# Seven half-size products for both feed-forward outputs, over neighbouring block pairs, three of them inside the input stage

## The chip, the core and the metric

The kernel runs on one core of a Trainium2 chip. The metric is the device time of one execution in microseconds. Engines are TensorE (PE, matmuls and weight loads), VectorE (DVE), ScalarE (ACT), GpSimd (POOL) and SyncE (SP, which issues most DMAs). Each engine takes its instructions in the order in which the program lists them and waits on semaphores for others. POOL and ACT can issue DMAs too.

## The reference

One layer over 512 tokens of width 1024 (D), with a feed-forward width FF of 2816 = 22 blocks of 128, all in fp32:

```python
mod = silu(c) @ w_ada + b_ada
sh1, sc1, g1, sh2, sc2, g2, sh3, sc3, g3 = split(mod, 9)
swiglu = lambda u, w_in, w_out: (silu(a) * b) @ w_out      # a, b = split(u @ w_in, 2)

u = rms_norm(x, ffn1_norm_g) * (1 + sc1) + sh1
x = x + 0.5 * g1 * swiglu(u, ffn1_w_in, ffn1_w_out)
u = rms_norm(x, mix_norm_g) * (1 + sc2) + sh2
merged = mix(u)               # mLSTM branch and forgetting attention, gated
x = x + g2 * (merged @ w_out)
u = rms_norm(x, ffn2_norm_g) * (1 + sc3) + sh3
x = x + 0.5 * g3 * swiglu(u, ffn2_w_in, ffn2_w_out)
```

## The kernel before

Every fp32 operand of a matmul is split into a high part (made by ACT, a copy to the matmul's type) and a low part (made by DVE, the difference). Each product is then three matmuls: high x high, low x high, high x low (`mm3`, L112 to L114; L93 and L95 split weights). Tiles ending in h and l, as wh and wl, are these parts. A weight tile is loaded by SP into raw, split, and used once. A matmul of 128x512 is the usual piece.

The stages, one after another: start (modulation rows 0 and 1, first norm, and blocks 0 to 2 of FFN1's input product), FFN1's input product for blocks 3 to 21, FFN1's output product, the mix, the branches, w_out, FFN2.

**FFN1.** `ffn_in` makes for each block j the two halves a and b (48 matmuls), then `ffn_h` makes silu(a) * b and stores its high and low part (hh, hl) in memory for all 22 blocks. `token_gemm` then computes the output in two halves of 512 columns: for each, 22 blocks x 4 token blocks x 3 matmuls. While this runs, x stays in its eight tiles, and `residual` adds to it. `ada_row` computes a row of the modulation on DVE (8 products of a 128x1024 weight, then a small matmul); rows 2 to 6 run as `extra` beside FFN1's input product, rows 7 and 8 beside its output product. The second norm's first half (`norm_half(0)`) runs in the last part of `token_gemm`, its second half behind it.

**FFN2** already uses seven half-size products (the Strassen-Winograd form of a 2x2 by 2x2 block product). The token rows are cut in two halves, the hidden blocks in pairs (j, j + 11), the output columns in two halves. With A the hidden values (A12: first token half, second block) and B the weights (B12: first block, second column half), sums are formed:

```
S1 = A21 + A22   S2 = S1 - A11   S3 = A21 - A11   S4 = A12 - S2
T1 = B12 - B11   T2 = B22 - T1   T3 = B12 - B22   T4 = B21 - T2
```

and the products are A11 B11, A12 B21, S1 T1, S2 T2, S4 B22, S3 T3, A22 T4. `pair_sums` forms the S on DVE, `weight_sums` the T: it loads the pair's two weight rows (tile rw, two buffers each 512 KB), splits B11 and B21, forms T1 and T2 with their parts and T3 and T4, and stores them to DRAM (T_d). A11 B11 and A12 B21 run inside the pairs (`first_products`, 12 matmuls a pair). The five others run behind the last pair in `ffn_out`, each 66 matmuls x 2 half-size outputs (`product`), with the T read back, T1 and T2 already split (`w_ready`). x stays in its tiles throughout.

The order on each engine follows the program's order as a scheduler laid it out; the names in the tables below are the program's, with a running number.

Of the kernel before, what the change touches and what calls it, by code (L numbers as in the profile page):

```python
# [20 lines left out]
P = 128  # L21
# [27 lines left out]
class Layer:  # L49
# [168 lines left out]

    def xn_start(self, pool):
        return [pool.tile([P, 512], F32, name=self.nm("xn"), tag="xs", bufs=8) for h in range(2)]  # L220
# [36 lines left out]
    def norm_half(self, hf, pool, G, sh):  # L257

        nc = self.nc
        if hf == 0:  # L260
            self.u_tiles()
        xn = self.xnorm(hf, pool)

        b = [self.tbank() for _ in range(4)]
        for k in range(NK):
            for i in range(2):
                nc.tensor.transpose(b[k % 4][:, k // 4 * 256 + i * P:k // 4 * 256 + (i + 1) * P],
                                    xn[i][k // 4][:, k % 4 * P:(k % 4 + 1) * P], self.ident)
        for k in range(NK):
            self.u_from(b[k % 4][:, k // 4 * 256:(k // 4 + 1) * 256], k, hf * 256, 256, G[:, k:k + 1], sh[:, k:k + 1], pool)  # L270
# [8 lines left out]
    def ada_row(self, v, pool, bank):  # L279

        nc, A = self.nc, self.A
        acc = pool.tile([P, D], F32, name=self.nm("acc"), tag="xn", bufs=2)
        br = pool.tile([1, D], F32, name=self.nm("br"), tag="xn", bufs=2)
        for k in range(NK):
            r = self.raw([P, D], [(lambda t: t, A["w_ada"][0, k * P:(k + 1) * P, v * D:(v + 1) * D])])
            if k == 0:
                nc.sync.dma_start(br, A["b_ada"][:, v * D:(v + 1) * D])
                with self.tc.issue_after(self.last_ul.ins):
                    nc.vector.tensor_scalar(acc, r, self.ccol[:, 0:1], None, op0=MUL)
            else:  # L290
                nc.vector.scalar_tensor_tensor(acc, r, self.ccol[:, k:k + 1], acc, op0=MUL, op1=ADD)  # L291
            if k == NK - 1:

                t = self.wp.tile([P, D], F32, name=self.nm("fo"), tag="wh", bufs=4)
                hl = self.wp.tile([P, D], F32R, name=self.nm("hl"), tag="wl", bufs=4)
                nc.scalar.activation(t[0:64, :], acc[64:P, :], AF.Copy)
                nc.vector.tensor_tensor(acc[0:64, :], acc[0:64, :], t[0:64, :], op=ADD)
                nc.scalar.activation(hl[0:64, :], acc[0:64, :], AF.Copy)
                nc.vector.tensor_tensor(hl[64:P, :], acc[0:64, :], hl[0:64, :], op=SUB)
                for h in range(2):  # L300
                    b = bank()
                    s = slice(h * 512, (h + 1) * 512)
                    nc.tensor.matmul(b[0:1, :], self.oneR, hl[:, s], start=True, stop=True)
                    nc.vector.tensor_tensor(br[:, s], b[0:1, :], br[:, s], op=ADD)
                nc.sync.dma_start(self.mod_d[v:v + 1, :], br)
            yield
# [20 lines left out]
    def ffn_h(self, ps_a, ps_b, j, c0, c1, hp, tp):  # L327
        nc = self.nc
        w = c1 - c0
        s = self.tmp(tp, "sl")  # L330
        nc.scalar.activation(s[:, :w], ps_a[:, c0:c1], AF.Silu)
        nc.vector.tensor_tensor(s[:, :w], ps_b[:, c0:c1], s[:, :w], op=MUL)
        nc.scalar.activation(self.hh[j][:, c0:c1], s[:, :w], AF.Copy)
        nc.vector.tensor_tensor(self.hl[j][:, c0:c1], s[:, :w], self.hh[j][:, c0:c1], op=SUB)

    def h_tiles(self, hp):
        self.hh = [hp.tile([P, T], F32R, name=self.nm("hh"), tag=f"hh{j}", bufs=1) for j in range(NJ)]
        self.hl = [hp.tile([P, T], F32R, name=self.nm("hl"), tag=f"hl{j}", bufs=1) for j in range(NJ)]

    def ffn_in(self, w_in, j0, hp, tp, extra=None):  # L340
        for j in range(j0, NJ):
            pa, pb = self.gbank(), self.gbank()
            self.gemm_stat(pa, self.w_stat(w_in, j * P), 0, T)
            self.gemm_stat(pb, self.w_stat(w_in, FF + j * P), 0, T)
            self.ffn_h(pa, pb, j, 0, T, hp, tp)
            self.lo_after = None
            if extra:
                extra(j)

    def ffn_in_halves(self, w_in, nj, hp, tp):  # L350

        wa = [self.w_stat(w_in, j * P) for j in range(nj)]
        wb = [self.w_stat(w_in, FF + j * P) for j in range(nj)]
        pp = [(self.gbank(), self.gbank()) for _ in range(nj)]
        for h in range(2):
            for j in range(nj):
                c0, c1 = h * 256, (h + 1) * 256
                self.gemm_stat(pp[j][0], wa[j], c0, c1)
                self.gemm_stat(pp[j][1], wb[j], c0, c1)
                self.ffn_h(pp[j][0], pp[j][1], j, c0, c1, hp, tp)  # L360

    def sum_tiles(self, hp):

        self.hc = {n: hp.tile([P, NP, 256], F32, name=self.nm(n), tag="hc", bufs=4) for n in ("S1", "S2", "S3", "A22")}
        self.s4 = [hp.tile([P, NP, 256], F32R, name=self.nm("s4"), tag=f"s4{i}") for i in range(2)]
        self.T_d = [self.dp.tile([NP * P, 1024], F32, name=self.nm("T_d")) for _ in range(3)]
        self.pair = {}

    def hidden(self, ps_a, ps_b, j, c0, c1, hp, tp):

        nc = self.nc
        jj, o = j % NP, 2 * (1 - j // NP)
        if jj not in self.pair:
            self.pair[jj] = hp.tile([P, 4, 256], F32, name=self.nm("hp"), tag="hp", bufs=2)
        h = self.pair[jj].rearrange("p c t -> p (c t)")[:, o * 256 + c0:o * 256 + c1]
        s = self.tmp(tp, "sl")
# [3 lines left out]
    def pair_sums(self, jj, hp):  # L380

        nc, V, h = self.nc, self.nc.vector, self.pair[jj]
        A12, A22, A11, A21 = (h[:, c, :] for c in range(4))
        c = {n: t[:, jj, :] for n, t in self.hc.items()}
        V.tensor_tensor(c["S1"], A21, A22, op=ADD)
        V.tensor_tensor(c["S2"], c["S1"], A11, op=SUB)
        V.tensor_tensor(c["S3"], A21, A11, op=SUB)
        nc.scalar.activation(c["A22"], A22, AF.Copy)
        hi = hp.tile([P, 2, 256], F32R, name=self.nm("ha"), tag="ha", bufs=2)
        lo = hp.tile([P, 2, 256], F32R, name=self.nm("la"), tag="la", bufs=2)  # L390
        nc.scalar.activation(hi, h[:, 0::2, :], AF.Copy)
        V.tensor_tensor(lo, h[:, 0::2, :], hi, op=SUB)
        V.tensor_tensor(A12, A12, c["S2"], op=SUB)
        nc.scalar.activation(self.s4[0][:, jj, :], A12, AF.Copy)
        V.tensor_tensor(self.s4[1][:, jj, :], A12, self.s4[0][:, jj, :], op=SUB)
        self.pair[jj] = (hi, lo)

    def weight_sums(self, w, jj, hp):

        nc, V = self.nc, self.nc.vector  # L400
        sh = [P, 1024]
        r1, r2 = (hp.tile(sh, F32, name=self.nm("rw"), tag="rw", bufs=2) for _ in range(2))
        nc.sync.dma_start(r1, w[jj * P:(jj + 1) * P, :])
        nc.sync.dma_start(r2, w[(jj + NP) * P:(jj + NP + 1) * P, :])
        B11, B12, B21, B22 = r1[:, 0:512], r1[:, 512:], r2[:, 0:512], r2[:, 512:]
        tiles = lambda: (self.wp.tile([P, 2, 512], F32R, name=self.nm("wh"), tag="wh", bufs=4),
                         self.wp.tile([P, 2, 512], F32R, name=self.nm("wl"), tag="wl", bufs=4))
        wh, wl = tiles()
        for i, B in enumerate((B11, B21)):
            nc.scalar.activation(wh[:, i, :], B, AF.Copy)  # L410
            V.tensor_tensor(wl[:, i, :], B, wh[:, i, :], op=SUB)
        self.pair[jj] += (wh, wl)
        V.tensor_tensor(B11, B12, B11, op=SUB)
        V.tensor_tensor(B12, B12, B22, op=SUB)
        V.tensor_tensor(B22, B22, B11, op=SUB)
        V.tensor_tensor(B21, B21, B22, op=SUB)
        th, tl = tiles()
        for i, B in enumerate((B11, B22)):
            nc.scalar.activation(th[:, i, :], B, AF.Copy)
            V.tensor_tensor(tl[:, i, :], B, th[:, i, :], op=SUB)  # L420
        rows = slice(jj * P, (jj + 1) * P)
        for d, t in zip(self.T_d, (th, tl)):
            nc.sync.dma_start(d[rows, :], t.rearrange("p i n -> p (i n)").bitcast(F32))
        nc.sync.dma_start(self.T_d[2][rows, 0:512], B12)
        nc.sync.dma_start(self.T_d[2][rows, 512:], B21)
# [18 lines left out]
    def product(self, ps, A, W, first, tail=0):  # L444
# [14 lines left out]
        for part in body:  # L459
            ops = (*A(*part), *W(*part))  # L460
            for t in range(2):
                run(t, part, ops)
# [840 lines left out]
```

## Time and profile before

| what | us |
|---|---|
| median of 3 runs (1366.8 to 1372.09) | 1367.05 |
| the profiled execution | 1370.4 |
| its span | 1368.6 |
| PE busy in the span | 1337.8 |
| start stage ends, FFN1's block 3 begins | 72.9 |
| FFN1's output product | 283.6 to 410.0 |
| branch stage | 876.0 to 964.5 |
| FFN2's pairs and closing products | 1011 to 1368.6 |

The span is the time from the first to the last instruction of the profiled execution; the 1.8 us beside it lie around it. PE is busy in all but 30.8 us of it, nearly half of which (14.6) lie in the first 76 us.

### The profile page before, as it was taken

How to read it: one execution, taken by the hardware profiler on the slowest of the kernel's cores; microseconds unless marked ns; L12 is line 12 of the kernel's file. 1: busy time of each engine (PE TensorE's matmuls, PEld its weight loads, DVE VectorE, ACT ScalarE, POOL GpSimd, SP SyncE). 2: the span in 40 equal slices, each digit the busy share in tenths (PEclk: the TensorE clock that was granted, in tenths of full speed). 3: DMA queues.
4: the chain of work that ended last, by engine and by line, in shares of the span. 5: the costliest groups of instructions: out<-in, count | busy, mean ns of one | idle time of the engine just before them, and what ended most of it. 6: DMA issues, size and time to landing. Idle time of an engine off the chain costs nothing.

```text
span 1368.6 us, 17759 instructions
## 1 busy us (share of the span) xinstructions
PE 1337.8 (98%) x6504; PEld 1118.9 (82%) x6504; DVE 874.2 (64%) x1567; ACT 596.8 (44%) x1034; POOL 115.4 (8%) x143
## 2 busy tenths in 40 slices
PE   6899999999999999999999999899999999999998
PEld 5788887888779888888888878788888888888787
DVE  6666666655548767867595876446566555565646
ACT  4433333322235755456465675332353333333343
POOL 2000000000002010313130411002010000000000
PEclk9899999999999999999999999999999999999999
DMA  9466666655634334343333253355326656556774
GB/s 315 134 200 191 184 198 206 217 188 179 223 85 104 117 101 131 112 131 120 108 101 112 81 154 94 92 166 174 126 74 218 213 162 223 185 188 212 245 274 150
DMA packets 226763, 221.92 MB, mean 162 GB/s; under 512 B 12082, under 2 KB 179666, under 8 KB 226676
## 3 DMA queue, kind: packets, MB, share of 16 engines
q1 hardware_dynamic: 226196, 220.71, 51.9%
q8 instruction: 51, 0.84, 0.2%
q14 instruction: 36, 0.29, 0.1%
q0 software_dynamic: 416, 0.06, 0.0%
q10 hardware_dynamic: 64, 0.02, 0.0%
HBM read 192.89 MB, written 27.86 MB: 161 GB/s over the span
## 4 chain that ended last, share of the span: by engine, by line
PE 85%; DVE 8%; ACT 3%; DMA 3%; issue 1%; SPq 0%; POOL 0%; POOLq 0%; DVEq 0%; ACTq 0%
PE g L114 21%; PE g L112 21%; PE g L113 21%; PE t L112 2%; PE t L113 2%; PE t L114 2%; PE g L709 2%; PE t L1051 2%; DVE wl L95 1%; PE t L456 1%; PE t L457 1%; PE t L455 1%; PE t L1021 1%; DMA wl<-T_d 1%; PE t L992 1%
## 5 line engine op out<-in xcount | busy, mean ns | idle before, releaser
L95 DVE TENSOR_TENSOR wl<-raw,wh 128x1024 fp32r<-128x1024 f32 (+2 forms) x217 | 275.7, 1271 | 185.6 <-ACT wh L93 164.5
L93 ACT ACTIVATE wh<-raw 128x1024 fp32r<-128x1024 f32 (+2 forms) x217 | 226.1, 1046 | 336.4 <-PE g L113 140.6
L114 PE MATMUL g<-uh,wl 128*128 128x512 f32 (+2 forms) x984 | 369.7, 376 | 2.1 <-DVE wl L95 2.1
L112 PE MATMUL g<-uh,wh 128*128 128x512 f32 (+2 forms) x984 | 370.8, 377 | 0.1
L113 PE MATMUL g<-ul,wh 128*128 128x512 f32 (+2 forms) x984 | 369.7, 376 | 0.0
L114 PEld LDWEIGHTS g<-uh,wl 128*128 128x128 f32 (+1 forms) x984 | 184.6, 188 | 37.3 <-DVE wl L95 3.3
L112 PEld LDWEIGHTS g<-uh,wh 128*128 128x128 f32 (+1 forms) x984 | 184.7, 188 | 34.1 <-ACT wh L93 1.1
L113 PEld LDWEIGHTS g<-ul,wh 128*128 128x128 f32 (+1 forms) x984 | 184.8, 188 | 33.6
L112 PE MATMUL g<-wh,uh 128*128 128x512 f32 (+1 forms) x320 | 111.8, 349 | 0.0
L114 PE MATMUL g<-wh,ul 128*128 128x512 f32 (+1 forms) x320 | 111.1, 347 | 0.0
L113 PE MATMUL g<-wl,uh 128*128 128x512 f32 (+1 forms) x320 | 111.0, 347 | 0.0
L291 DVE SCALAR_TENSOR_TENSOR acc<-raw,ccol,acc 128x1024 f32<-128x1024 f32 x49 | 62.8, 1282 | 13.0 <-DMA raw<-in_w_ada_dram 12.3
L112 PEld LDWEIGHTS g<-wh,uh 128*128 128x128 f32 x320 | 60.5, 189 | 7.8 <-DVE tk L905 0.5
L114 PEld LDWEIGHTS g<-wh,ul 128*128 128x128 f32 x320 | 60.5, 189 | 7.8
L113 PEld LDWEIGHTS g<-wl,uh 128*128 128x128 f32 x320 | 60.5, 189 | 7.4
L112 PE MATMUL g<-yh,wh 128*128 128x512 f32 x128 | 50.1, 395 | 3.7 <-ACT yh L1110 3.7
L254 POOL TENSOR_TENSOR ul<-uf,uh 128x256 fp32r<-128x256 f32 x16 | 13.5, 846 | 456.0 <-DVE uf L253 456.0
L114 PE MATMUL g<-yh,wl 128*128 128x512 f32 x128 | 50.5, 395 | 0.0
L113 PE MATMUL g<-yl,wh 128*128 128x512 f32 x128 | 50.3, 393 | 0.0
L378 DVE TENSOR_TENSOR hp<-g,sl 128x512 f32<-128x512 f32 (+1 forms) x24 | 15.4, 646 | 51.5 <-PE g L114 50.9
L1003 ACT ACTIVATE S<-S,mn 128x128 f32<-128x128 f32 (+1 forms) x64 | 35.6, 557 | 22.5 <-DVE mn L995 14.8
L984 POOL TENSOR_TENSOR Am<-A,maskF 128x512 f32<-128x512 f32 x16 | 24.0, 1500 | 136.4 <-DMA A<-A_d 133.6
(316 smaller groups left out, 2215.1 us busy)
## 6 DMA issues: line engine op xcount, KB each, us to landing
raw<-in_ffn_w_in_dram SPq DMA_DIRECT2D x82, 512.0 KB
raw<-in_w_ada_dram SPq DMA_DIRECT2D x56, 512.0 KB
raw<-in_w_mix_dram SPq DMA_DIRECT2D x48, 512.0 KB
raw<-in_ffn_w_out_dram SPq DMA_DIRECT2D x27, 512.0 KB
rw<-in_ffn_w_out_dram SPq DMA_DIRECT2D x22, 512.0 KB
raw<-in_w_mix_dram SPq DMA_DIRECT2D x32, 256.0 KB
ar<-in_w_ada_dram SPq DMA_DIRECT2D x14, 512.0 KB
T_d<-rw SPq DMA_DIRECT2D x22, 256.0 KB
```

The lines of the kernel that those rows point to most:

```text
L93: nc.scalar.activation(hi, src, AF.Copy)
L95: self.last_lo = (eng or nc.vector).tensor_tensor(lo, src, hi, op=SUB)
L112: mm(ps, lh, rh, start=start, stop=False)
L113: mm(ps, lh, rl, start=False, stop=False)
L114: self.last_mm = mm(ps, ll, rh, start=False, stop=stop)
L291: nc.vector.scalar_tensor_tensor(acc, r, self.ccol[:, k:k + 1], acc, op0=MUL, op1=ADD)
L378: nc.vector.tensor_tensor(h, ps_b[:, c0:c1], s[:, :c1 - c0], op=MUL)
L455: mm(ps[t], a[0], wh[:, k, :], start=first and c + k == 0, stop=False, skip_group_check=True)
L709: mm = nc.tensor.matmul(acc_ps[b], (wl if p == 1 else wh)[:, b % 2, s], ul if p == 2 else uh, start=k == 0 and p == 0, stop=k == NK - 1 an ...
L984: nc.gpsimd.tensor_tensor(b4(Am), b4(A0), self.maskF[:, None, :].to_broadcast([P, NT, P]), op=ADD)
L1003: nc.scalar.activation(S[:, ws], S[:, ws], AF.Exp, scale=-1.0, bias=m, accum_out=sm[:, qb:qb + 1])
L1051: nc.tensor.matmul(po[:, q0:], vt[pr][:, kb, i % 2, :], Px[:, o:o + T - q0], start=n == 1, stop=n == 8)
```

## The change

Both FFNs now go through one path. FFN1's output becomes seven half products (462 matmuls for 528), and in both the pair is (2jj, 2jj + 1), so that a pair is complete one block after the other.

- `first_products` runs three products per pair inside the input stage (18 matmuls): S1 T1 is added to the two. Its operands ah, al, s1, th, tl take the eight tiles of x. FFN1 therefore fetches x again from the input, FFN2 stores x to x_d before its pairs and fetches it back, by DMAs on POOL's queue (`x_again`), which also fetches the broadcast gate row.
- `weight_load` loads a pair's weights by one 1 MB DMA into rw, with one buffer; `weight_sums` forms T1 to T4 in place; `sums_store` stores 768 KB of them (T3, T4, T2, as plain fp32) to S_d. The next pair's load waits for that store.
- `pair_out` runs the four other products: S2 T2, S4 B22, S3 T3, A22 T4, splitting the weights as they are read.
- Modulation rows 2 to 5 stay beside FFN1's pairs (`ada_steps`), 6 and 7 move to the branch stage, 8 to FFN2's pairs.
- The second norm is cut into `norm_scale` and `norm_turn`, which are hooked into FFN1's closing products; the first half of the mix's q and k product now runs between the two halves of the norm.

```diff
+    def pair_sums(self, jj):
+        nc, V, h = self.nc, self.nc.vector, self.pair.pop(jj)
+        A12, A22, A11, A21, S1 = (h[:, c, :] for c in range(5))
+        S2 = self.s2[:, jj, :]
+        i = 3 * (jj % 2)
+        ah, al, s1 = (self.xslot([P, 2, 256], i + n) for n in range(3))
+        nc.scalar.activation(ah, h[:, 0:3:2, :], AF.Copy)
+        V.tensor_tensor(S1, A21, A22, op=ADD)
+        V.tensor_tensor(al, h[:, 0:3:2, :], ah, op=SUB)
...
+        V.tensor_tensor(A12, A12, S2, op=SUB)
+        nc.scalar.activation(self.ph[:, jj], h[:, 0:3, :], AF.Copy)
+        V.tensor_tensor(self.pl[:, jj], h[:, 0:3, :], self.ph[:, jj], op=SUB)
+    def weight_load(self, w, jj):
+        r = self.fp.tile([P, 2, 1024], F32, name=self.nm("rw"), tag="rw", bufs=1)
+        self.nc.sync.dma_start(r, w[2 * jj * P:2 * (jj + 1) * P, :].rearrange("(two p) n -> p two n", p=P))
+        self.wsum[jj] = r
+    def weight_sums(self, jj):
+        r = self.wsum[jj]
+        B11, B12, B21, B22 = (r[:, i // 2, i % 2 * 512:(i % 2 + 1) * 512] for i in range(4))
...
+        nc.scalar.activation(wh, r[:, :, 0:512], AF.Copy)
+        V.tensor_tensor(wl, r[:, :, 0:512], wh, op=SUB)
+        V.tensor_tensor(B11, B12, B11, op=SUB)
+        th, tl = (self.xslot([P, 512], 6 + n) for n in range(2))
+        nc.scalar.activation(th, B11, AF.Copy)
+        V.tensor_tensor(B12, B12, B22, op=SUB)
+        V.tensor_tensor(B22, B22, B11, op=SUB)
+        V.tensor_tensor(tl, B11, th, op=SUB)
+        V.tensor_tensor(B21, B21, B22, op=SUB)
+    def sums_store(self, jj, r):
+        self.nc.sync.dma_start(self.S_d[jj * P:(jj + 1) * P, :], r.rearrange("p two n -> p (two n)")[:, 512:2048])
     def first_products(self, jj):
...
         for i, ps in ((1, self.pa), (0, self.pb)):
-            self.mm_pair(ps, hi[:, i, :], lo[:, i, :], wh[:, 1 - i, :], wl[:, 1 - i, :], jj == 0, jj == NP - 1)
+            self.mm_pair(ps, ah[:, i, :], al[:, i, :], wh[:, 1 - i, :], wl[:, 1 - i, :], *ends)
+        self.mm_pair(self.pc, s1[:, 0, :], s1[:, 1, :], th, tl, *ends)
+    def x_again(self, src):
+        self.x_tiles()
+        for half, tbs in ((0, (0, 1)), (1, (0, 1)), (1, (2, 3)), (0, (2, 3))):
+            for tb in tbs:
+                self.nc.gpsimd.dma_start(self.x[tb][half], src[tb * P:(tb + 1) * P, half * 512:(half + 1) * 512])
+    def pair_out(self, w, v, src, final, hooks={}):
...
+        nc.gpsimd.dma_start(g, self.mod_d[v:v + 1, :].to_broadcast([P, D]))
+        self.x_again(src)
...
+        def first_out():
+            for t in range(2):
+                add(t, 0, self.pb[t], p1[:, t, :])
...
+        for t in self.product(a, self.a_split(self.s2), self.w_split(sums, 1024), False, 0, {2: first_out}):
+            px = px or snap()
+            copy(px[:, t, :], a[t], AF.Copy)
+        for t in self.product(c, self.a_ready(0), self.w_split(last, 512), False):
+            add(t, 1, c[t], px[:, t, :])
+        for t in self.product(a, self.a_ready(2), self.w_split(sums, 0), False, 2, hooks):
+            add(2 + t, 1, a[t], p5[:, t, :])
+        for t in self.product(a, self.a_ready(1), self.w_split(sums, 512), False, 2):
+            add(2 + t, 0, a[t])
+    def ffn_pairs(self, w_in, w_out, j0, steps, n):
         for jj in range(NP):
+            first = lambda: 0 < jj < NP - 1 and self.first_products(jj - 1)
+            if 2 * jj >= j0:
+                self.block(w_in, 2 * jj)
+            self.weight_load(w_out, jj)
+            if 2 * jj >= j0:
+                first()
+                steps(True, n)
+            r = self.weight_sums(jj)
+            if 2 * jj + 1 >= j0:
+                self.block(w_in, 2 * jj + 1)
+            if 2 * jj < j0 <= 2 * jj + 1:
+                first()
+            self.sums_store(jj, r)
+            self.pair_sums(jj)
+            if jj:
+                steps(2 * jj < j0, n)
+        self.first_products(NP - 2)
+        steps(True, 9)
         self.first_products(NP - 1)
```

j0 is 3 in FFN1 (blocks 0 to 2 come from the start stage) and 2 in FFN2 (`first_pair` makes blocks 0 and 1 by token halves).

The order on ACT where FFN1's pairs begin, before: Silu and high parts (hh) of blocks 0 to 2; wh_737 and wh_767 are the weights of block 3.

```order
L93 ACTIVATE wh_737<-raw_735 128x1024
L93 ACTIVATE wh_767<-raw_765 128x1024
L331 ACTIVATE sl_718<-g_190 128x512
L331 ACTIVATE sl_723<-g_192 128x512
L331 ACTIVATE sl_728<-t_194 128x512
L333 ACTIVATE hh_674<-sl_718 128x512
```

The same place after: rw_689 and rw_717 are the output weights of pairs 0 and 1, xs and ph are parts of pair 0's hidden values and sums, wh_735 and wh_765 the weights of block 3.

```order
L371 ACTIVATE sl_686<-t_194 128x512
L409 ACTIVATE wh_691<-rw_689 128x1024
L384 ACTIVATE xs_704<-hp_678 128x512
L387 ACTIVATE xs_706<-hp_678 128x256
L413 ACTIVATE xs_696<-rw_689 128x512
L392 ACTIVATE ph_674<-hp_678 128x768
L409 ACTIVATE wh_719<-rw_717 128x1024
L93 ACTIVATE wh_735<-raw_733 128x1024
L93 ACTIVATE wh_765<-raw_763 128x1024
```

Block 3's weights stood ahead of the Silus; they now stand behind the split of pair 1's output weights.

On PE, before, block 3 (g_733, weights wh_737) follows the last matmuls of the start stage (t_195):

```order
L709 MATMUL t_195<-uh_181,wl_620 128x512
L709 MATMUL t_195<-ul_189,wh_619 128x512
L112 MATMUL g_733<-uh_174,wh_737 128x512
L113 MATMUL g_733<-ul_182,wh_737 128x512
L114 MATMUL g_733<-uh_174,wl_738 128x512
```

After, pair 0's first two products (t_796 to t_799, 12 matmuls, of which the last are shown) stand between, and block 3 is g_731:

```order
L431 MATMUL t_798<-wh_691,xs_705 128x512
L430 MATMUL t_799<-wl_692,xs_704 128x512
L431 MATMUL t_799<-wh_691,xs_705 128x512
L112 MATMUL g_731<-uh_174,wh_735 128x512
L113 MATMUL g_731<-ul_182,wh_735 128x512
L112 MATMUL g_732<-uh_174,wh_765 128x512
L114 MATMUL g_731<-uh_174,wl_736 128x512
```

Twelve matmuls that stood later now come first there.

On DVE where FFN2's first pair is summed, before: rw_9409 and rw_9410 are the pair's weights, wl_9438 the low part of the next block's.

```order
L411 TENSOR_TENSOR wl_9414<-rw_9409,wh_9413 128x512
L413 TENSOR_TENSOR rw_9409<-rw_9409 128x512
L414 TENSOR_TENSOR rw_9409<-rw_9409,rw_9410 128x512
L411 TENSOR_TENSOR wl_9414<-rw_9410,wh_9413 128x512
L415 TENSOR_TENSOR rw_9410<-rw_9410,rw_9409 128x512
L420 TENSOR_TENSOR wl_9424<-rw_9409,wh_9423 128x512
L416 TENSOR_TENSOR rw_9410<-rw_9410 128x512
L420 TENSOR_TENSOR wl_9424<-rw_9410,wh_9423 128x512
L95 TENSOR_TENSOR wl_9438<-raw_9435,wh_9437 128x1024
```

After, with rw_9634 the pair's weights and wl_9667 the next block's low part (block 2):

```order
L410 TENSOR_TENSOR wl_9637<-rw_9634,wh_9636 128x1024
L411 TENSOR_TENSOR rw_9634<-rw_9634 128x512
L414 TENSOR_TENSOR rw_9634<-rw_9634 128x512
L372 TENSOR_TENSOR hp_9469<-g_9418,sl_9572 128x256
L415 TENSOR_TENSOR rw_9634<-rw_9634 128x512
L416 TENSOR_TENSOR xs_9642<-rw_9634,xs_9641 128x512
L417 TENSOR_TENSOR rw_9634<-rw_9634 128x512
L95 TENSOR_TENSOR wl_9667<-raw_9664,wh_9666 128x1024
```

The first product of the row now takes both halves of the weights in one 128x1024 operation from a single tile, and the next block's low part still stands behind the sums.

More of the change, by code (lines that the diff above doesn't have):

```diff
@@ L340, in ffn_in @@
[L340 to L360, printed above, removed]
@@ L398, in weight_sums, with xslot @@
-    def weight_sums(self, w, jj, hp):
-        nc, V = self.nc, self.nc.vector
[L401 to L412, printed above, removed]
+    def xslot(self, shape, tag):
+        return self.xp.tile(shape, F32R, name=self.nm("xs"), tag=f"x{tag}")
```

332 lines of the change are left out of this document (158 added, 174 removed).

## The prediction

> **What bounds the kernel now.** I read the page first, then the waits of TensorE, then a table of windows by stage. The page's line of busy times and its chain:
>
> ```profile
> PE 1337.8 (98%) x6504; PEld 1118.9 (82%) x6504; DVE 874.2 (64%) x1567; ACT 596.8 (44%) x1034; POOL 115.4 (8%) x143
> PE 85%; DVE 8%; ACT 3%; DMA 3%; issue 1%; SPq 0%; POOL 0%; POOLq 0%; DVEq 0%; ACTq 0%
> ```
>
> PE is busy 1337.8 of 1368.6 us, so all its idle time is 30.8 us. Time falls only if PE gets fewer or denser matmuls, and every new hole in PE is paid in full. The waits of PE (engine, line, waited-for, total us, times, longest) that lie near the change:
>
> ```profile
> PE g L709 <- ACT uh L249: 4.4, 4, 1.4
> PE g L114 <- DVE wl L95: 2.1, 4, 1.1
> PE g L456 <- DMA wl<-T_d: 1.8, 2, 1.3
> ```
>
> Only the third belongs to something removed (sums read back ready split). The windows: start and end, length, busy time and count by engine, clock, DMA share, GB/s:
>
> ```profile
> 76.00:283.60 207.60, 206.35 (x908) 169.05 (x908) 132.38 (x132) 70.02 (x84) 0.00 (x0) 1.00 0.64 199
> 290.00:340.00 50.00, 50.00 (x216) 40.07 (x215) 26.57 (x24) 12.68 (x13) 0.00 (x0) 1.00 0.60 200
> 1100.00:1150.00 50.00, 50.00 (x222) 41.41 (x221) 28.82 (x43) 17.55 (x26) 0.00 (x0) 1.00 0.59 190
> 1312.00:1362.00 50.00, 50.00 (x222) 41.38 (x221) 31.77 (x38) 23.39 (x30) 0.00 (x0) 1.00 0.56 188
> ```
>
> All four stages are PE-bound, at full clock (1.00), with DMA at 0.56 to 0.64 and DVE at about 60%: what the change puts on those two is free until it orders PE to wait. FFN1's output product (290–340) places 216 matmuls in 50 us, 0.2315 us apart; FFN2's pairs and its closing products place 222, 0.2252 apart.
>
> **What is removed.** FFN1's output is 8 half products, 2 halves x 22 blocks x 4 token blocks x 3 = 528 matmuls; seven are 462. At the densities above: 528 x 0.2315 = 122.2 us against 462 x 0.2252 = 104.0, **−18.2 us**. If the new products kept the old density it would be 66 x 0.2315 = −15.3. I take −18.2, since the new code is FFN2's form. FFN2 had seven products already: there only the read-back wait goes, **−1.8**.
>
> **What is added at the start of FFN1 (place A).** Three blocks come ready from the start stage, so pairs 0 and half of 1 exist before block 3. Each pair takes a 1 MB load into rw, of which there is one; the sums are formed in it, stored (768 KB), and only then may the next load begin. Every engine takes its instructions in the order printed above, so a waiting one holds all behind it. ScalarE now has the high part of pair 1's weights (tile wh_719) ahead of that of block 3's (wh_735), and PE, after 12 matmuls of pair 0, wants wh_735. In the profile of before PE passes this place without a gap (start and duration in us, engine, line, what is made from what, and in brackets the idle time before and who ended it); the last four rows are from FFN2 and give DVE's pace:
>
> ```profile
> 72.39 0.60 ACT L331 ACTIVATE sl<-t 128x512 f32<-128x512 f32 x1 [1.11 <-PE t L709]
> 72.88 0.39 PE L112 MATMUL g<-uh,wh 128*128 128x512 f32 x1
> 73.15 0.69 DVE L332 TENSOR_TENSOR sl<-t,sl 128x512 f32<-128x512 f32 x1 [0.84 <-PE t L709]
> 74.45 1.05 ACT L93 ACTIVATE wh<-raw 128x1024 fp32r<-128x1024 f32 x1
> 75.56 1.22 DVE L95 TENSOR_TENSOR wl<-raw,wh 128x1024 fp32r<-128x1024 f32 x1
> 76.69 1.28 DVE L291 SCALAR_TENSOR_TENSOR acc<-raw,ccol,acc 128x1024 f32<-128x1024 f32 x1
> 1036.09 0.69 DVE L415 TENSOR_TENSOR rw<-rw,rw 128x512 f32<-128x512 f32 x1
> 1036.69 0.69 DVE L420 TENSOR_TENSOR wl<-rw,wh 128x512 fp32r<-128x512 f32 x1
> 1041.89 0.42 DVE L387 TENSOR_TENSOR S<-hp 128x256 f32<-128x256 f32 x1
> 1042.23 0.42 DVE L393 TENSOR_TENSOR hp<-hp,S 128x256 f32<-128x256 f32 x1
> ```
>
> So DVE's pace is 1.13 us for a 128x1024, 0.60 for a 128x512, 0.34 for a 128x256. Pair 0's load can be issued at about 64.7, when the start stage frees its memory, and lands before 72, so it holds nobody. ACT splits pair 0's weights and hidden values from 73.0 (the last Silu's end) to 74.7, and PE's 12 matmuls fill 74.7 to 77.4. DVE's last hidden product ends at 73.15 + 0.69 = 73.8. From there its order to the last sum of pair 0 holds one 128x1024, six 128x512 (the last to its end) and three 128x256: 1.13 + 5 x 0.60 + 0.69 + 3 x 0.34 = 5.8, so the store leaves at 79.7. The prices of store and load:
>
> ```profile
> 1028.98 0.42 SPq L404 DMA_DIRECT2D rw<-in_ffn_w_out_dram  x1
> 1028.59 0.34 SPq L403 DMA_DIRECT2D rw<-in_ffn_w_out_dram  x1
> 1028.98 5.80 DMA rw<-in_ffn_w_out_dram
> 1032.16 0.63 ACT L410 ACTIVATE wh<-rw 128x512 fp32r<-128x512 f32 x1 [2.09 <-DMA rw<-in_ffn_w_out_dram]
> 1057.08 0.56 SPq L425 DMA_DIRECT2D T_d<-rw  x1
> 1060.88 0.33 SPq L404 DMA_DIRECT2D rw<-in_ffn_w_out_dram  x1
> 1039.03 0.40 SPq L425 DMA_DIRECT2D T_d<-rw  x1
> 1043.24 0.33 SPq L404 DMA_DIRECT2D rw<-in_ffn_w_out_dram  x1
> ```
>
> Two 512 KB loads took from 1028.59 to 1034.8, some 6.0 us for 1 MB; the first alone 3.6, my lower end; 8 with other loads beside it, my upper. From a store out of rw to the load that waited for it: 3.8 and 4.2, I take 4.0 (3.4 to 4.5). Then: load issued 83.7, landed 89.7; pair 1's weights on ACT to 90.8 (1.05 each), block 3's two to 91.8 and 92.9; on DVE pair 1's low part to 92.0, block 3's to 93.1. PE flows from 93.0. It has done pair 0's 12 matmuls and three of block 3 by then, 15 x 0.227 = 3.4 (0.227 apart, from 72.20 in the rows further down to 72.88 above in three steps). Loss: 93.0 − 72.9 − 3.4 = **+16.7**, from 13.7 (short ends) to 19.2 (long ends). Nothing covers it, since PE has no other work ahead of block 3. Behind the waiting instructions stand, on ACT, block 3's and 4's weights, on DVE block 3's low part, on SP the next weights' loads; these are early enough, as PE itself is late.
>
> The clock adds to it. The trace shows what PE does behind holes:
>
> ```profile
> 66.61 0.63 PE L709 MATMUL g<-uh,wl 128*128 128x512 f32 x1
> 71.31 0.59 PE L709 MATMUL t<-uh,wh 128*128 128x512 f32 x1
> 72.20 0.39 PE L709 MATMUL t<-uh,wh 128*128 128x512 f32 x1
> ```
>
> Behind holes that sum to 2 us between 62.6 and 66.0, twelve matmuls, the first and last of which are shown, start 0.427 us apart ((71.31 − 66.61) / 11) and not 0.227: they lose 12 x 0.2 = 2.4. A hole of some 15 us should do the same: **+2.5** (0 to 5, if a second slow stretch follows). The Trainium skill, "TensorE: Matmul & The Clock Gate", Part 1, has the array fall to half clock after an idle window of about 3.4 us and need about as much busy time to come back; by that rule the loss is half of 3.4, 1.7 us, and the sum would be 0.8 lower. The 4.7 us of slow rows here are longer than that, and the sum goes by the rows.
>
> **At the start of FFN2 (place B)** ready weights stand behind the sums, on DVE:
>
> ```profile
> 1034.88 0.69 DVE L414 TENSOR_TENSOR rw<-rw,rw 128x512 f32<-128x512 f32 x1 [0.62 <-DMA rw<-in_ffn_w_out_dram]
> 1037.68 0.40 PE L113 MATMUL g<-ul,wh 128*128 128x512 f32 x1
> 1038.49 1.22 DVE L95 TENSOR_TENSOR wl<-raw,wh 128x1024 fp32r<-128x1024 f32 x1
> 1039.77 0.50 PE L114 MATMUL g<-uh,wl 128*128 128x512 f32 x1 [0.58 <-DVE wl L95]
> ```
>
> PE now reaches the first low part of block 2 at 37.9 (no first product stands ahead of it). DVE holds it behind pair 0's sums: load landed 34.8, ACT to 35.9, low part to 37.1, then five 128x512 and a 128x256 to 40.5, then block 2's own to 41.7. PE waits 3.8, against 0.6 now: **+3.2** (0.5 to 4). At pair 1, the load that follows pair 0's store lands near 52 and block 3's low part is ready near 55.5, while PE arrives near 56: 0.
>
> **Steady pairs.** A pair is 96 + 18 matmuls x 0.227 = 25.9 us. The rw circle is 6.0 + 1.05 + 5.9 + 4.0 = 17, so some 5 us are over after queueing. DVE has per pair 7.3 of sums, 4.5 of low parts, 1.2 of hidden products and four adaptation products of 1.28, 18 of 25.9. On SP, weight loads stand behind the rw load that waits for its store, 4 us per pair, as they do behind L404 in FFN2 before, where PE didn't wait: 0. The extra 2 MB of x that FFN2 stores go out before its first pair's load, beside the norm, whose DMA has room: 0.
>
> **The closing stage.** x is fetched again on POOL's queue once the last first products have freed its slots. Such transfers show:
>
> ```profile
> rowsA<-in_b_mix_dram POOLq DMA_DIRECT2D x2, 4.0 KB, 5.2
> rowsA<-in_mix_norm_g_dram POOLq DMA_DIRECT2D x1, 4.0 KB, 4.2
> rowsA<-in_fox_k_norm_g_dram POOLq DMA_DIRECT2D x1, 4.0 KB, 5.8
> 2.91 0.54 POOL L156 DMA_DIRECT2D rowsA<-in_conv_w_dram  x1
> 3.44 0.54 POOL L156 DMA_DIRECT2D rowsA<-in_conv_b_dram  x1
> ```
>
> Issue to landing 4.2 to 5.8, issues 0.53 apart, so several are under way together. Counted from the end of the last first product: three issues 1.5, landing 5 more, two adds 1.2, fourth chunk's low part 1.1, together 8.5 to 9; PE wants that part after three chunks of 12 matmuls, 8.2. About 0.5 in each FFN, **+1** (0 to 3 each).
>
> **Rows 6 and 7 of the modulation** move beside the branches:
>
> ```profile
> 876.00:964.50 88.50, 88.49 (x383) 73.07 (x384) 50.13 (x53) 28.69 (x37) 9.01 (x7) 0.98 0.51 163
> ```
>
> 16 products of 1.28 and two tails add some 25 us to DVE's 50 of 88, and 8 MB of loads take 163 GB/s to about 258. PE stays the longer one: **+1** (0 to 4). FFN1's input stage loses row 6 in exchange. Norm, transposes and the half of the q and k product that moves ahead of the second turn are the same instructions in another order, with the same inputs ready: 0 (−1 to +1).
>
> **Sum**: −18.2 − 1.8 + 16.7 + 2.5 + 3.2 + 1 + 1 = **+4.4 us** on the profiled run's 1370.4, that is 1374.8. That run is 3.3 above the median of the runs, 1367.05; on the median it is **1371.5**. Its own bounds: short ends −20.0 + 13.7 + 0.5 = −5.8; long ends −15.3 + 19.2 + 5 + 4 + 10 = +23, hardly all at once.
>
> **Rivals.** *Slower, x comes late.* In each closing stage DVE holds the two adds that need x ahead of the fourth chunk's low part. Should POOL's transfers go one after another instead of together, broadcast row, then three pieces of x, 4 x 4.7 = 19 us pass instead of 6.5: PE stands 12 in each FFN, or 6 if they half overlap: +12 to +24, 1383 to 1395. It decides from a landing over 8 us behind the issue. For it: these pieces are 256 KB and not 4, and DVE is busy all through. Against it: those at the start of before overlapped. The Trainium skill, "SBUF — State Buffer", section "SBUF: two separate sides", warns that transfers issued from POOL starve while DVE holds the shared port; no row of before shows POOL's queue beside a busy DVE. Chance 0.25.
> *Faster, A is short.* If store and load need little more than 2 us each beside an idle chip and the clock holds, A is 10, B is 1: −20 + 11 = −9, 1358. The 3.6 us of half such a load speak against. That block 3 were not behind pair 1's weights would take A away altogether, 1350; the order of ScalarE speaks against. Chance 0.15 for both.
> *Not denser.* The new products run at 0.2315: +2.9, 1374.5, within the forecast.
>
> **Numbers.** Forecast, that the hole at A eats the gain: 0.60, mostly 1365 to 1379. A measurement tells about 0.5%, 6.8 us. Of the forecast's 0.60 some 0.12 lies above +6.8: faster 0.15, same 0.48, slower 0.37. The range 1357 to 1386 leaves out the faster case's 1350 and the worse half of the late x.
>
> **What would show it.** Right: in the profile after, PE has one hole near 77–92 behind pair 0's 12 matmuls, released by ACT at block 3's first weights, 128x512 matmuls 0.63 us long behind it; another of 3 to 4 us at FFN2's second block, released by DVE; windows of the closing products hold 222 in 50 us. Wrong: PE seamless at 77; or holes in each pair (the circle too long); or waits on x in the closing stages.

## The result, and the profile after

| | median us | range | runs |
|---|---|---|---|
| before | 1368.28 | 1366.59 to 1372.09 | 6 |
| changed | 1376.76 | 1375.0 to 1382.57 | 6 |

The ratio is 1.0065, with a 95% interval of 1.0042 to 1.0088: the changed kernel is slower by 6 to 12 us, where +4.4 had been forecast. Its profiled execution took 1375.0 us, with a span of 1373.1.

The end of the start stage moves from run to run (72.9 us in the profile of before, 70.8 in that of after, 67.1 to 71.7 in the others), so stages are compared below from there. From the end of the start stage's last matmul (counted as 0.227 us behind its start) to the end of the span, before takes 1295.7 us and after 1302.3: **+6.6**. The 1.9 us between this and the 8.5 of the medians are not traced to a stage: one run of each kernel has a trace.

The page's busy times and the waits of PE after (engine, line, waited-for, total us, times, longest), those of the start stage left out:

```profile
PE 1322.4 (96%) x6438; PEld 1107.3 (81%) x6438; DVE 938.7 (68%) x1699; ACT 618.8 (45%) x1050; POOL 125.0 (9%) x161
```

```profile
PE g L112 <- ACT wh L93: 12.9, 1, 12.9
...
PE g L112 <- ACT sl L371: 4.0, 1, 4.0
PE g L112 <- ACT yh L1133: 3.1, 2, 2.6
PE t L456 <- DVE rs L517: 2.9, 3, 2.3
...
PE g L112 <- DVE br L316: 2.2, 4, 0.5
...
PE t L429 <- ACT xs L384: 1.5, 1, 1.5
```

PE is busy 15.4 us less than before, 66 matmuls at work, but its idle time grew from 30.8 to 50.7 us. The largest hole is where it was expected. The timeline of after there (start, duration, engine, line, what; idle time before and who ended it):

```profile
77.57 0.34 SPq L422 DMA_DIRECT2D S_d<-rw  x1
81.20 0.38 SPq L399 DMA_DIRECT2D rw<-in_ffn_w_out_dram  x1
86.35 1.06 ACT L409 ACTIVATE wh<-rw 128x1024 fp32r<-128x1024 f32 x1 [7.59 <-DMA rw<-in_ffn_w_out_dram]
87.31 2.94 ACT L93 ACTIVATE wh<-raw 128x1024 fp32r<-128x1024 f32 x3
88.41 0.79 PE L112 MATMUL g<-uh,wh 128*128 128x512 f32 x1 [12.92 <-ACT wh L93]
89.00 0.63 PE L113 MATMUL g<-ul,wh 128*128 128x512 f32 x1
92.16 0.44 PE L113 MATMUL g<-ul,wh 128*128 128x512 f32 x1
92.43 0.39 PE L114 MATMUL g<-uh,wl 128*128 128x512 f32 x1
```

The chain reads from top to bottom: pair 0's sums leave rw, pair 1's load may start 3.6 us later, lands after 5.2, ACT splits it, and only then block 3's weights, for which PE had stood since 75.5. Behind the hole eight steps take 3.75 us instead of 1.8, a loss of 1.9.

At FFN2's start there is a hole too, but another one than was predicted:

```profile
1027.37 0.42 DVE L260 TENSOR_TENSOR ul<-uf,uh 128x256 fp32r<-128x256 f32 x1
1027.53 0.83 POOL L260 TENSOR_TENSOR ul<-uf,uh 128x256 fp32r<-128x256 f32 x1 [0.41 <-DVE uf L259]
1027.85 1.28 ACT L371 ACT_TABLE_LOAD   x1 [2.03 <-issue]
1029.15 0.66 ACT L371 ACTIVATE sl<-g 128x256 f32<-128x256 f32 x2
1029.59 0.58 PE L112 MATMUL g<-uh,wh 128*128 128x256 f32 x1 [4.04 <-ACT sl L371]
1029.96 0.41 PE L113 MATMUL g<-ul,wh 128*128 128x256 f32 x1
1034.23 0.32 PE L112 MATMUL g<-uh,wh 128*128 128x256 f32 x1
1040.53 2.35 DVE L95 TENSOR_TENSOR wl<-raw,wh 128x1024 fp32r<-128x1024 f32 x2
```

PE waits for the first Silu. ACT holds in front of it until VectorE has ended the norm's last subtraction on that engine (1027.79), then loads the Silu's table for 1.28 us, and POOL's last subtraction (to 1028.36) ends within that load. In before the first Silu stood at 1015.97, ahead of the norm's second half. Then 21 matmuls come 0.22 us apart instead of 0.12 (1029.59 to 1034.23), 2.1 us. The last row is the low part of block 2's weights: its first half ends at 1041.7, as predicted, but PE comes there late itself and doesn't wait.

### The profile page after: what moved, and what is told of

It reads as the page before. It is cut to its first block, busy times and chain, and to the rows that moved or that the text cites. A ratio compares the mean times of both kernels' runs of the same rounds, so it can differ in the third digit from the quotient of the medians.

```text
span 1373.1 us, 17882 instructions
## 1 busy us (share of the span) xinstructions
PE 1322.4 (96%) x6438; PEld 1107.3 (81%) x6438; DVE 938.7 (68%) x1699; ACT 618.8 (45%) x1050; POOL 125.0 (9%) x161
## 5 line engine op out<-in xcount | busy, mean ns | idle before, releaser
L93 ACT ACTIVATE wh<-raw 128x1024 fp32r<-128x1024 f32 (+2 forms) x225 | 232.3, 1037 | 359.6 <-PE g L113 122.1
L112 PE MATMUL g<-uh,wh 128*128 128x512 f32 (+2 forms) x984 | 373.0, 380 | 19.1 <-ACT wh L93 12.9
L299 DVE SCALAR_TENSOR_TENSOR acc<-raw,ccol,acc 128x1024 f32<-128x1024 f32 (+1 forms) x63 | 66.6, 1077 | 36.7 <-DMA raw<-in_w_ada_dram 36.5
L372 DVE TENSOR_TENSOR hp<-g,sl 128x512 f32<-128x512 f32 (+1 forms) x45 | 29.7, 665 | 50.7 <-PE g L114 49.5
L409 ACT ACTIVATE wh<-rw 128x1024 fp32r<-128x1024 f32 x22 | 23.3, 1058 | 72.6 <-PE g L113 45.2
L410 DVE TENSOR_TENSOR wl<-rw,wh 128x1024 fp32r<-128x1024 f32 x22 | 26.9, 1221 | 27.7 <-ACT wh L409 27.7
```

The source lines that it names most:

```text
L93: nc.scalar.activation(hi, src, AF.Copy)
L112: mm(ps, lh, rh, start=start, stop=False)
L299: nc.vector.scalar_tensor_tensor(a, r[:, cut(i)], self.ccol[:, k:k + 1], a, op0=MUL, op1=ADD)
L372: nc.vector.tensor_tensor(h, ps_b[:, c0:c1], s[:, :c1 - c0], op=MUL)
L409: nc.scalar.activation(wh, r[:, :, 0:512], AF.Copy)
L410: V.tensor_tensor(wl, r[:, :, 0:512], wh, op=SUB)
```

## The experiments

All start from the changed kernel unless another is named. "Rest" is the time from the end of the start stage to the end of the span in the profiled execution.

| run | median us | ratio to before, 95% | rest |
|---|---|---|---|
| changed | 1376.76 | 1.0065 (1.0042 to 1.0088) | 1302.3 |
| block 3 first | 1369.99 | 1.0013 (0.9997 to 1.0029) | 1297.3 |
| sums behind each second block | 1368.35 | 1.0008 (0.9994 to 1.0022) | 1295.2 |
| FFN2's temporaries in their own pool | 1376.02 | 1.0061 (1.0037 to 1.0085) | 1303.3 |
| 54 extra matmuls | 1381.27 (one run) | | 1309.8 |
| 74 extra matmuls | 1382.36 (one run) | | 1308.5 |
| late turn | 1371.57 (one run) | | 1302.1 |
| before, 32 bytes | 1366.39 | 0.9983 (0.9972 to 0.9994) | 1295.6 |
| before, 96 bytes | 1368.1 | 0.9992 (0.998 to 1.0004) | 1295.7 |
| four edits, 32 bytes | 1359.81 | 0.9933 (0.9915 to 0.995) | 1289.6 |
| four edits, 96 bytes | 1359.92 | 0.9927 (0.991 to 0.9945) | 1290.7 |

**Block 3 ahead of pair 1's weights.**

```diff
+            mid = 2 * jj < j0 <= 2 * jj + 1
+            if mid:
+                self.block(w_in, 2 * jj + 1)
             self.weight_load(w_out, jj)
...
-            if 2 * jj + 1 >= j0:
+            if 2 * jj + 1 >= j0 and not mid:
                 self.block(w_in, 2 * jj + 1)
```

> The changed kernel with one move: in FFN1's second pair, block 3 is written ahead of the load and the sums of pair 1's output weights, so that ScalarE splits block 3's weights before it waits for pair 1's. Theory (the hole at the start of FFN1 comes from the order on ScalarE behind the single rw buffer): the holes of 12.92 and 1.47 us at 72 to 88 us and the slow matmuls behind them (about 2 us) go, so the time falls by 13 to 17 us from 1376.8, to about 1360 to 1364, below the kernel before (1368.3). A small new hole of up to 4 us may show at pair 2, whose rw load now follows closer. Rival (the rw circle itself is too slow for the stage): the wait comes back at the next pairs, and less than 5 us are gained: 1372 or more.

The hole of 12.92 is gone, but the time fell by 6.8 us, half of what was expected. The timeline of its PE shows what came instead:

```profile
79.03 0.50 PE L114 MATMUL g<-uh,wl 128*128 128x512 f32 x1 [1.29 <-DVE wl L95]
90.69 0.50 PE L112 MATMUL g<-uh,wh 128*128 128x512 f32 x1 [1.35 <-ACT wh L93]
98.02 0.50 PE L114 MATMUL g<-uh,wl 128*128 128x512 f32 x1 [1.07 <-DVE wl L95]
...
109.96 0.50 PE L114 MATMUL g<-uh,wl 128*128 128x512 f32 x1 [0.52 <-DVE wl L95]
...
346.71 0.50 PE L457 MATMUL t<-wl,ah 128*128 128x512 f32 x1 [1.71 <-DVE wl L95]
```

So both theories were partly right: the order made the hole, and the stage behind it had been fed while PE stood in that hole. With it closed, ACT and DVE are late at the first pairs, and in the closing stage the fourth chunk's low part is late by 1.7. That is the wait foreseen for the transfers on POOL's queue, which the profile of after doesn't show; here VectorE stood 2.29 us for the gate row among them, not for x.

**Sums behind each second block, in all pairs.**

```diff
-            r = self.weight_sums(jj)
             if 2 * jj + 1 >= j0:
                 self.block(w_in, 2 * jj + 1)
+            r = self.weight_sums(jj)
```

> The changed kernel with the sums of each pair's output weights written behind the pair's second block, for all pairs of both FFNs, so that no block's weights stand behind a pair's weights on ScalarE or VectorE while the rw load is late. Theory (what the first reordering left, seven waits of 0.3 to 1.7 us that sum to 7.1, most of them are the same order at pairs 1 and 2): of those at 79 to 110 us at most 2 us stay, and it gains 3 to 5 us more than the first reordering (1370.0), about 1365 to 1367. Rival (they come from VectorE, which has too much to do while it catches up, in whatever order): the waits stay at 5 us or more, 1369 to 1371.

The waits between 78 and 110 us are 1.30, 1.22 and 0.28, together 2.8 and not at most 2, and the median fell by 1.6, which its interval can't tell from none; the rest fell by 2.0. Between the two theories: the order carried the waits at pairs 1 and 2, but three others, where PE waits for a bank that the modulation's tail holds (L316), grew from 0.55 to 1.55, 1.09 and 1.55, so part of VectorE's lateness moved. And behind the wait of 1.22 the granted clock is 0.50 from 91.2 to 94.6 us, a loss of 1.9 that the first reordering doesn't have.

**FFN2's temporaries in a pool of their own.**

```diff
-        with tc.tile_pool(name="f2", bufs=1) as fp:
-            self.tp = fp
+        with tc.tile_pool(name="f2t", bufs=1) as tp, tc.tile_pool(name="f2", bufs=1) as fp:
+            self.tp = tp
```

> The changed kernel with one edit at FFN2: its temporaries (sl among them) get a pool of their own that is opened first, as before the change; they then lie where no tile of the branch stage lies. Theory (the 4.04 us wait of PE at 1029.6 is for a Silu that waits for the last subtraction of the norm on GpSimd, only because its output lies in memory of the pool which the norm still uses): that wait goes, and with it about 2 us of slow matmuls behind it; in its place the wait that was predicted there, for the low part of block 2's weights behind pair 0's sums on VectorE, of up to 4 us can show. Net 2 to 6 us less: 1371 to 1375. Rival (the Silu waits for VectorE's and ScalarE's own norm work, not for memory): the wait stays at 4 us, no change from 1376.8.

The wait for the Silu is gone, and no matmul there is slow. From the norm's transposes (1005.63 after, 1009.61 here) to the end it takes 364.3 us and not 367.5: 3.2 less, at the low end of the theory, since smaller waits (0.89 at pair 1, 0.96 in the closing stage) came up. The median doesn't show it, because in this run's profile the hole at FFN1's start is 15.26 us and not 12.92, with nothing changed there: the load on which it hangs landed later. That the Silu waited for memory and not for the norm's result is shown, as nothing in the program but the place of its output was changed. The scheduler then also lays the first Silu ahead of the norm's second half, as in before:

```profile
1019.76 0.39 ACT L371 ACTIVATE sl<-g 128x256 f32<-128x256 f32 x1
```

The wait that had been predicted here didn't come in its place either: on VectorE the low part of block 2's weights now stands ahead of most of pair 0's sums and is ready at 1040.9, before PE wants it at 1041.7.

**Extra matmuls in the hole.** Their results are overwritten.

```diff
+        if j == NJ0 and not hasattr(self, "warm"):
+            self.warm = True
+            for _ in range(54):
+                self.nc.tensor.matmul(pa, self.uh[0][:, 0:P], self.uh[1], start=True, stop=True)
```

> The changed kernel with 54 extra matmuls of 128x512, whose results are overwritten, on PE ahead of pair 0's first products, so that PE is busy in most of the hole at the start of FFN1. Theory (the matmuls of 0.63 us behind the hole are the clock's answer to idle PE): block 3 still begins at about 88.4 us, but its matmuls are 0.39 us long and 0.227 apart from the first, and about 2 us are gained. Rival (the slow matmuls come from the waiting operands or from DMA beside them): they stay 0.63 us long.

> As the run with 54 extra matmuls, with 74, since 54 left an idle time of 4.25 us, behind which the matmuls were again 0.63 us long. Theory (the clock falls for idle PE and for nothing else): the hole ahead of block 3 is under 2 us, and its matmuls are 0.39 us long from the first. Rival (waiting operands or DMA): 0.63 us all the same.

With 54, PE still idled 4.25 us, and the matmuls behind were 0.63 us long. With 74, PE idled 1.74 us, and this is its timeline:

```profile
91.51 0.50 PE L112 MATMUL g<-uh,wh 128*128 128x512 f32 x1 [1.74 <-ACT wh L93]
91.84 0.40 PE L113 MATMUL g<-ul,wh 128*128 128x512 f32 x1
92.80 0.63 PE L113 MATMUL g<-ul,wh 128*128 128x512 f32 x1
95.36 0.63 PE L113 MATMUL g<-ul,wh 128*128 128x512 f32 x1
96.21 0.39 PE L112 MATMUL g<-uh,wh 128*128 128x512 f32 x1
```

The first matmuls were fast, then eight were slow, with the operands there and no idle time between. Operands are thus no cause. DMA isn't one either: the granted clock is 0.50 in the slow stretch and 1.00 behind it, where the DMA share is higher (0.89 for 0.61; the windows stand in the last section). So it is the clock, but a hole shorter than 2 us was enough, against the expectation; in the changed kernel the hole of 2.27 us at 394 has no slow matmuls behind it (the next are 0.40 us long). What decides is shown in the last section. The runs took 1381.3 and 1382.4 us, single runs, longer than the changed kernel: the extra matmuls stood ahead of pair 0's first products, and block 3 began no earlier.

**The norm's turn in the fourth closing product.**

```diff
-                self.pair_out(A["ffn1_w_out"][0], 2, A["x"][0], False, {0: scale, 3: turn})
+                self.pair_out(A["ffn1_w_out"][0], 2, A["x"][0], False, {0: scale}, {0: turn})
```

> The changed kernel with the second norm's first turn hooked into the fourth closing product of FFN1 instead of the third. Theory (the 2.27 us hole ahead of the fourth product comes from VectorE, which finishes the turn's subtractions before it reads the third product's bank): that hole is under 0.5 us, 2 us gained in the stretch between 380 and 420 us. Rival (the bank is read late because the third product's end itself releases it late): the hole stays at 2.3 us. By the medians alone 2 us can't be told.

In the changed kernel PE has its 2.27 us hole at 394.04, where DVE, behind twelve operations of the turn, reads the third product's bank. Here the same border of the products has no such hole:

```profile
389.18 0.39 PE L458 MATMUL t<-wh,pl 128*128 128x512 f32 x1
389.51 0.50 PE L456 MATMUL t<-wh,ph 128*128 128x512 f32 x1
```

The hole is gone, as the theory said, and from the first closing matmul to the branch stage it takes 528.3 us instead of 529.8. But the rest is 1302.1, as in the changed kernel: a wait for yh in the branch stage grew from 0.56 to 1.38, and the stages ahead of the closing products took 0.5 more. The lower time of this single run, 1371.57 us, is the start stage's, which ended 3.2 us earlier.

**Addresses.** In the changed kernel's FFN1, the closing products that read ph and pl have matmuls of 395 ns, and those in FFN2 389, by the same code (groups by tile, ns min, median, max; first the window of FFN1, then of FFN2):

```profile
L456 PE MATMUL g<-wh,ph x22: 392/395/396, 358.7 to 373.4; 128*128 128x512 f32 x22
...
L456 PE MATMUL g<-wh,ph x22: 389/389/389, 1322.0 to 1336.3; 128*128 128x512 f32 x22
```

So density isn't the form's. What was suspected next is the address at which FFN1's tiles begin (32 bytes off a multiple of 64, which no profile shows), and so there are two tries on the kernel before:

```diff
             self.consts(tp)
+            nc.vector.memset(tp.tile([P, 8], F32, name="pad"), 0.0)
```

> The kernel before with one 32-byte tile put ahead of FFN1's hidden tiles (hh, hl), so that these begin at multiples of 64 bytes and no longer 32 bytes off. Theory (matmuls whose operand begins 32 bytes off a multiple of 64 are 0.233 us apart and not 0.227, which is why FFN1's output product was less dense than all others, and the changed kernel's ph and pl in FFN1 as well): the 528 matmuls of FFN1's output come 0.2267 apart, 395 ns becomes 389, and the time falls by 3.5 us to about 1365. Rival (the density belongs to the form of that product, as the prediction took it): they stay at 0.233, no change from 1368.3.

> The kernel before with 96 bytes put ahead of FFN1's hidden tiles. With 32 bytes these began at a multiple of 128 bytes, and their matmuls stayed 395 ns long, so that the theory of multiples of 64 fell. What is left of it: in all matmuls of 389 ns both operands begin 64 bytes past a multiple of 128 (the weights always do), and in those of 395 ns the hidden values began 96 or 0 bytes past one. Theory (the operands' addresses must agree modulo 128 bytes): now hh and hl begin 64 past a multiple of 128, their matmuls are 389 ns long and 0.227 us apart, and FFN1's output product takes 123 us and not 126.4. Rival (not the address): 395 ns and 126.4 us again.

The second with 24 in place of 8. Its matmuls on hh:

```profile
L112 PE MATMUL t<-wh,hh x88: 387/395/398, 281.9 to 343.2; 128*128 128x512 f32 x88
L113 PE MATMUL t<-wl,hh x88: 392/395/399, 282.1 to 343.5; 128*128 128x512 f32 x88
```

Both theories of addresses fell: some 395 ns, and 126.6 and 126.4 us for the product. The lower median with 32 bytes (ratio 0.9983) doesn't come from the product that the edit was meant for: in its profile the rest is 1295.6, as in before.

**The edits together.** The sums behind each second block, the pool of their own and the late turn, with the 32 bytes in the first kernel and the 96 in the second.

> The four edits together: sums behind each pair's second block, FFN2's temporaries in a pool of their own, FFN1's hidden tiles at multiples of 64 bytes, the norm's turn in the fourth product. Theory (the losses are separate holes of PE, which add): 12.9 + 2 at the start less 3 that stay, 3.2 at FFN2's start, 1.3 from 198 matmuls 6.6 ns closer, 2.2 at the turn, together 17 to 19 less than 1376.8, about 1358 to 1361, below the kernel before (1368) and below it with the alignment alone (1366.4). Rival (one hole closed opens the next, as in the first reordering): 1364 or more.

> The four edits together with 96 bytes in place of 32. Theory of addresses: FFN1's 198 closing matmuls that read ph and pl are 389 ns long, 1.3 us less than with 32 bytes (1359.8), about 1358.5, which the medians can't tell apart but the trace can. Rival: 395 ns again, 1359.8.

1359.81 and 1359.92 us: 17 us less than the changed kernel, within the range of the theory, and faster than the kernel before by 0.5 to 0.9%. That the range was met is partly luck. The sum counted 1.3 us for the alignment, which gave nothing (393 to 396 ns in both), 2.2 for the turn, whose run alone left the rest where it was, and nothing for waits that would grow. And the rest fell by 12.7 and 11.6 us, not by 17; where the medians have the other 4 to 5 us from is not traced. The other three edits together carry the gain; no run tells their shares apart. The waits that stay in the first of the two, the first two larger than in the changed kernel:

```profile
PE g L112 <- DVE br L316: 4.8, 4, 1.6
...
PE g L112 <- ACT yh L1133: 4.4, 2, 2.6
...
PE g L112 <- ACT wh L93: 2.1, 2, 1.8
...
PE t L429 <- ACT xs L384: 1.5, 1, 1.5
PE g L114 <- DVE wl L95: 1.4, 2, 1.3
```

## Why the prediction was right, and where it wasn't

The forecast, that a hole at FFN1's start eats the gain of 66 matmuls, is what happened, at about twice its net size (+8.5 in the medians). Of its three signs the first came, a hole behind pair 0's matmuls with slow ones behind it. The second, a hole at FFN2's second block released by DVE, did not. The third, 222 matmuls in 50 us of a closing stage, came out at 215 in FFN1 (from 344 us) and 217 in FFN2 (from 1308), holes included. By its steps:

- **Matmuls, −18.2.** 264 of the new ones came at 0.2267 us, 198 at 0.2333 (the ph products in FFN1), against 528 at 0.2333 before: 123.2 − 106.0 = **−17.2**. The step took the lower density for a property of the old product's form; it isn't, and what it belongs to is open. So the rival *Not denser* came for these 198.
- **T_d's wait, −1.8.** Gone, and with it the 0.58 at FFN2's block 2.
- **Place A, +16.7.** 1.47 + 12.92 = **14.4**, the mechanism as put. The chain began 2 us earlier, as the start stage did; store to load took 3.6 for 4.0, the load 5.2 for 6.0 (the two rows that the 6.0 was read from give 6.2). The first reordering removed the hole, so the order is shown as its cause. That the single buffer sets when the load starts is read from the trace (store at 77.57, load at 81.20); no run gave it a second buffer.
- **Clock, +2.5 there.** 1.9. Not foreseen: another 2.1 behind FFN2's hole. A third slow stretch, 1.6 in the branch stage, stands in both kernels.
- **Place B, +3.2.** This step failed. DVE's chain came out as worked (1041.7), but a hole ahead of it had made PE late. The Silu's output now lies in memory of the branch stage's pool, so ScalarE must wait for the norm's last subtractions on VectorE and POOL, which the prediction didn't look for. It costs 4.04 + 2.1. That 4.04 lies near the 3.8 us forecast for the other wait is chance.
- **Closing stages, +1 for x.** The transfers took 5.7 and 6.0 us at the median:

```profile
x<-in_x_dram POOLq DMA_DIRECT2D x8, 256.0 KB, 5.7
x<-x_d POOLq DMA_DIRECT2D x8, 256.0 KB, 6.0
```

   PE didn't wait for them in after, so the term came out at 0 there. In six of the other runs it waited 0.2 to 1.7 us in FFN1 for the low part of the last weights (L457), within the term's bounds. Missed was the bank that DVE reads late, 2.27 + 0.67.
- **Rows 6 and 7, +1.** From the branch stage's first matmul to the norm of FFN2, 129.8 became 132.15: **+2.35**. By the trace 0.8 of it is waits for yh and yl (0.56 and 0.22), 0.9 the rows' four matmuls, which FFN1 no longer has; the rest isn't traced, and no run undid this step.
- **Banks held by the modulation's tail (L316)**, 2.2 in four waits, were missed. The changed kernel holds six of eight banks through the input stage.

The sum of what the trace shows: −17.2 − 2.3 (T_d, block 2) − 3.1 (waits of before that are gone: 1.12, 0.57, 0.28 and 1.1 of 3.67) + 14.4 + 1.9 + 6.1 (place B) + 2.9 and 2.2 (the late banks) + 0.6 (yh) + 0.6 (a wait for ul behind the second norm) = +6.1, against +6.6 in the rest. The forecast of +4.4 was low by the missed waits (the Silu, the bank that DVE reads late, L316). It came as near as it did because A and the clock came out 2.9 smaller and the waits that are gone, 3.1, had not been counted: that is luck. Its long bound of +23 leaves out the −1.8; with it, it is +21.

Of the rivals, *x comes late* didn't come: transfers from POOL overlapped, and 256 KB landed 5.7 us behind the issue (7.3 at most), with DVE busy 12.0 of 13.7 us in FFN1 and 10.9 of 14.5 in FFN2. The Trainium skill's warning ("SBUF — State Buffer", section "SBUF: two separate sides") is that transfers issued by POOL stall while VectorE runs an operation that takes both SBUF ports, as a float32 copy within SBUF does; no such stall shows in this trace, though how many of VectorE's operations there were of that kind was not measured. *A is short* fell with 14.4.

## What to carry to other kernels

Where a buffer is reused through a store and a load, look at what stands behind its consumer on every engine in program order: the weights queued behind one wait made a hole of 13 us, and with them moved ahead of it some 7 us of smaller waits came up. A hole hides the lateness of what follows, so a fix is priced by the next wait and not by the hole. When a pool moves, list the waits that its new neighbours bring, as with a Silu that came to wait for a norm through memory alone.

## What the runs showed of the hardware

- The granted clock in the window of the hole, with its DMA share and GB/s, last columns:

```profile
76.00:100.00 24.00, 11.59 (x43) 9.09 (x44) 13.04 (x17) 6.29 (x7) 0.00 (x0) 0.72 0.64 205
```

   Slow matmuls (0.63 us for 128x512, 0.41 for 128x256) followed the holes of 12.9, 4.25 and 4.04 us, but also one of 1.74. Behind a hole of 2.27 us ahead of FFN1's fourth closing product there are none in the changed kernel, and 3.4 us of them in the run with the own pool. The traces tell why. The clock that they record for the stages behind the start is 1.00 or 0.50, and each slow stretch ahead of the last matmul lasts 3.41 us or 2, 4 or 5 times that, on one grid through a whole run (in after they begin at 78.57, 873.88 and 1027.48, which is 233 and 45 steps of 3.413 apart). The windows of this grid at such holes (length, then PE's and PEld's busy time and count, and so on, granted clock, DMA share, GB/s), from after, from the run with the own pool and from the one with 74 extra matmuls:

```profile
392.59:396.01 3.42, 1.97 (x9) 1.63 (x10) 3.42 (x7) 0.56 (x1) 0.88 (x2) 1.00 0.02 5
396.01:399.42 3.41, 3.41 (x16) 2.78 (x15) 3.41 (x5) 2.34 (x5) 0.00 (x0) 1.00 0.51 169
...
395.83:399.24 3.41, 1.26 (x6) 1.06 (x7) 3.41 (x8) 1.27 (x2) 1.58 (x2) 1.00 0.01 5
399.24:402.65 3.41, 3.41 (x10) 2.63 (x9) 3.41 (x5) 1.55 (x5) 0.00 (x0) 0.50 0.43 159
...
89.38:92.79 3.41, 1.67 (x7) 0.97 (x6) 2.25 (x2) 2.96 (x3) 0.00 (x0) 1.00 0.00 0
92.79:96.21 3.42, 3.42 (x9) 2.61 (x8) 3.35 (x6) 0.00 (x0) 0.00 (x0) 0.50 0.61 168
96.21:99.62 3.41, 3.41 (x16) 2.81 (x15) 0.65 (x2) 0.00 (x0) 0.00 (x0) 1.00 0.89 318
```

   In after a border at 392.59 cut the hole in two, and PE was busy for 1.97 us of the window; with 1.26 and 1.67 the next window got half the clock. Over all twelve traces, between the start stage and the last matmul, every window at full clock in which PE idled 1.74 us or more has one at 0.50 behind it, and none in which it idled 1.49 or less; in between both occur. So about half a window of idle time decides, and where the grid lies, which differs from run to run. The Trainium skill ("TensorE: Matmul & The Clock Gate", Part 1) has the clock fall after an idle window of about 3.4 us, and the windows run freely. The grid agrees with that, but here about half a window of idle time was enough.
- Matmuls of FFN1's late products took 393 to 397 ns, those of both input products and of all of FFN2's 389, with no padding ahead of FFN1's tiles (as in before) as with 32 or 96 bytes of it. The cause is open.
- The 1 MB load at the start of FFN1 took 5.2 us in the changed kernel's trace and 7.5 in that of the run with the own pool, with nothing changed ahead of it.
